# A hybrid attention and FFN block: another step-by-step order of the recurrent chain under the projections, and a rearranged start of the FFN

## The chip, the cores and the metric

The kernel runs on the 8 cores of one Trainium2 chip (two dies of four cores); every core does one sequence of the batch. The metric is device time in microseconds (us) of the slowest core.

Such a program has a slow state in some of its executions, in which the cores of one die, or both, get a lower clock.

## The reference

One layer: a sliding-window attention branch and a gated linear attention branch (GLA) from one input projection, gated and merged, an output projection, and a SwiGLU FFN.

```python
D_MODEL, BATCH, SEQ, FFN_HIDDEN = 2048, 8, 2048, 5632
# 32 query heads of 64, 4 key/value heads, window 128; 4 GLA heads, dk 256, dv 512
u = _rmsnorm(h, norm1_w[l])
proj = u @ w_in[l]
aq, ak, av, gq, gk, gv, g_lr, g_r, gate_a, gate_b = jnp.split(proj, offs, axis=-1)
attn_o = _swa_sink_attention(aq, ak, av, attn_sinks[l])
# S_t = diag(alpha_t) S_{t-1} + k_t^T v_t ; o_t = q_t S_t / sqrt(dk)
gla_o = _gla(gq, gk, gv, log_a)                     # (reshapes left out)
gla_o = _rmsnorm(gla_o, gla_norm_w[l]) * jax.nn.silu(g_r)
h = h + (sigmoid(gate_a) * attn_o + sigmoid(gate_b) * gla_o) @ w_out[l]
v2 = _rmsnorm(h, norm2_w[l])
h = h + (silu(v2 @ w_ffn_gate[l]) * (v2 @ w_ffn_up[l])) @ w_ffn_down[l]
# after the layer: final RMSNorm
```

## The kernel before

Each core handles its sequence in two halves of 1024 tokens (`c` = 0, 1; 8 row tiles of 128 each). In a half, four heads follow one another: 16 attention projections (`a_proj`), then 32 projections for the GLA (`g_proj`), each 16 matmuls of 128x512, some 3.5 us. Under these the kernel lays short dependent chains: the attention chain under `g_proj`, and the GLA chain of a head under the attention projections of the *next* head. Chains and projections are generators; one `next()` emits one step.

The steps of the GLA chain give TensorE 0.23 or 1.30 us of work, but between two of its steps VectorE and ScalarE must do theirs (the row factor, the row `g_gn`), and then TensorE transposes `g_gn`. The weave spreads 19 steps over 16 projections:

```python
def weave(filler, overlay, n_fill, n_over):
    done = 0
    i = 0
    for _ in filler:
        i += 1
        want = min(n_over, (i * n_over) // n_fill)     # 19/16: two steps at i = 6, 11, 16
        while done < want:
            next(overlay, None)
            done += 1

gc = iter(())
for h in range(4):
    weave(a_proj(c, h), gc, 16, 19)
    for _ in gc:
        pass
    if c > 0:
        load(G["g_U"]..., sd[h], "ul", ("sd", h))      # this head's saved state
    ac, gp, gc = a_chain(c, h, range(NT)), g_proj(c, h), g_chain(c, h)
    if h < 3:
        weave(gp, ac, 32, 16)
# head 3: 24 projections with the attention chain (cut), then 8 with the GLA chain
for i in range(8):
    next(gp)
    next(gc)
...
rows_in(range(1, 5))                                   # residual rows of x, 1 MB a tile
dg = d_groups(c)                                       # output projection: one group = 16 matmuls + add
for i in range(11):
    next(gc, None)
    ...
    next(dg)
```

`d_groups` takes its column groups in the order (0, rows 0 to 3), (1, rows 0 to 3), (0, rows 4 to 7), and so on. While it does the last column groups it normalises finished rows (`norm_rows`, VectorE) and transposes them (`norm_turn`: TensorE transposes, ScalarE copies into `v2T`).

The FFN multiplies by Strassen's scheme: seven products `m` per pair of hidden blocks, each twice (`q` = 0, 1) with 8 matmuls; sums of weights (`wsum_part`) and of activations (`xs_add`) are VectorE's. The first pair starts while the last rows are still being normalised:

```python
def snap(bank):
    y = fbuf()                      # the first two of these lie on n2bc, the norm weights
    acopy(y[:], bank[:, :])
    return y

for m in order:                     # first pair: 4, 2, 5, 1, 3, 7, 6
    for q in range(2):
        if m == 4:
            product(A[q], wv[1][:, :, q, 1, :], xs4[:], True)
            m4[q] = snap(A[q])
        elif m == 2:
            product(B[q], wsx[:, 2, :, q, :], v[:, lo, t1], True)
            vtt(m4[q][:], B[q][:, :], m4[q][:], ALU.add)
            out(q, m4[q], 1, t1)    # Silu at q == 0
        elif m == 5:
            product(B[q], wsx[:, 1, :, q, :], v[:, hi, t2], True)
            m5[q] = snap(B[q])
        ...
```

The softmax here doesn't subtract the row's maximum and nothing guards it: scores larger than these inputs give would overflow.

## Time and profile before

| | before |
|---|---|
| median of 4 runs | 3921.66 us |
| fastest of them | 3680.57 us |
| profiled run, slowest core | 3694.52 us (span 3693.0) |
| spans of the 8 cores in it | 3652.6 to 3693.0 us |
| TensorE busy, slowest core | 3591.7 us (97%) |
| half-clock spells between 100 and 3580 us, all 8 cores | 50, costing 15.4 us a core |

The last row is from the clock records of all cores: a spell at half clock costs half its length. The slices round the clock to tenths, so spells of a few microseconds cannot be seen there.

### The profile page before, as it was taken

What the parts mean: (1) busy time and instruction counts of PE and PEld (TensorE: products, weight loads), DVE (VectorE), ACT (ScalarE), POOL (GpSimd) and SP (SyncE); (2) the same over time, 40 slices, a digit from 0 to 9 for tenths busy, and PEclk for the clock granted to TensorE, in tenths of its full rate; (3) what the DMA queues carried; (4) which work ended last, traced back from release to release, by engine and by line L of the source; (5) the groups of instructions that cost most, each with busy time, mean ns of one, the idle gap of its engine ahead of it and who ended that gap; (6) DMA issues with size and microseconds to landing.
All of it is one profiled execution on the core that took longest, in us unless ns stands there. A gap on an engine that the chain in (4) does not pass through costs nothing.

```text
span 3693.0 us, 47906 instructions; the slowest of 8 cores (3652.6 to 3693.0 us)
## 1 busy us (share of the span) xinstructions
PE 3591.7 (97%) x17464; PEld 1630.6 (44%) x17464; DVE 1620.1 (44%) x2589; ACT 1183.5 (32%) x2229; POOL 205.2 (6%) x370
## 2 busy tenths in 40 slices
PE   7999999999999999999999999999999999999997
PEld 5444444444444444444454444444444444444443
DVE  3134443444466513664113343444446674156623
ACT  3153544445333300221113535353533221012212
POOL 1000000000000000000000000000001000000000
PEclk8899999999999999999999999999999999999999
DMA  8344434355666688665954333333456577854464
GB/s 190 50 64 75 68 56 66 51 94 113 160 133 139 108 183 177 138 143 134 218 123 77 61 75 69 69 60 67 92 135 177 120 170 156 200 130 91 89 151 134
DMA packets 110907, 425.35 MB, mean 115 GB/s; under 512 B 13521, under 2 KB 19281, under 8 KB 75089
## 3 DMA queue, kind: packets, MB, share of 16 engines
q0 software_dynamic: 37584, 268.58, 41.3%
q1 hardware_dynamic: 73090, 153.69, 13.0%
q8 instruction: 142, 2.33, 0.3%
q14 instruction: 91, 0.75, 0.1%
HBM read 616.34 MB, written 65.02 MB: 185 GB/s over the span
## 4 chain that ended last, share of the span: by engine, by line
PE 88%; DMA 5%; DVE 3%; ACT 1%; issue 1%; POOL 1%; DVEq 0%; ACTq 0%; POOLq 0%; SPq 0%
PE ps L336 63%; PE ps L877 24%; DMA xnd<-sqh 2%; DMA sq<-xT 1%; PE ps L344 1%; PE ps L632 1%; DMA xr<-x 1%; DMA sq<-x 1%; DVE ws L369 0%; DVE fb L369 0%; DVE mT L380 0%; ACT tt L360 0%; DVE g_gn L380 0%; DVE g_U L380 0%; ACT g_Sb L360 0%
## 5 line engine op out<-in xcount | busy, mean ns | idle before, releaser
L336 PE MATMUL ps<-xnT,wu 128*128 128x512 bf16 (+1 forms) x3264 | 737.9, 384 | 7.9 <-DMA wu<-wmix 4.7
L336 PE MATMUL ps<-wu,xnT 128*128 128x512 bf16 (+1 forms) x3328 | 720.0, 375 | 0.0
L336 PE MATMUL ps<-wu,ff 128*128 128x512 bf16 x2816 | 608.4, 379 | 0.0
L336 PEld LDWEIGHTS ps<-xnT,wu 128*128 128x128 bf16 x3264 | 320.3, 100 | 401.8 <-issue 88.9
L336 PEld LDWEIGHTS ps<-wu,xnT 128*128 128x128 bf16 x3328 | 320.4, 99 | 384.6 <-issue 56.1
L336 PEld LDWEIGHTS ps<-wu,ff 128*128 128x128 bf16 x2816 | 275.4, 98 | 332.4
L877 PE MATMUL ps<-v2T,ws 128*128 128x512 bf16 x1408 | 323.8, 384 | 13.5 <-DVE ws L369 10.4
L877 PE MATMUL ps<-xs,wu 128*128 128x512 bf16 x1408 | 318.2, 379 | 3.2 <-DVE fb L369 2.6
L877 PE MATMUL ps<-v2T,wu 128*128 128x512 bf16 x1408 | 312.5, 379 | 8.1 <-DVE fb L369 5.1
L363 ACT COPY fb<-ps 128x512 f32<-128x512 f32 x264 | 150.5, 582 | 526.6 <-PE ps L877 517.9
L360 ACT ACTIVATE sg<-fb 128x512 bf16<-128x512 f32 x176 | 110.9, 630 | 552.3 <-DVE fb L369 551.0
L369 DVE TENSOR_TENSOR fb<-ps,fb 128x512 f32<-128x512 f32 x264 | 177.9, 688 | 158.9 <-PE ps L877 149.1
L336 PE MATMUL ps<-wu,mT 128*128 128x512 bf16 x1024 | 228.3, 382 | 0.0
L369 DVE TENSOR_TENSOR hy<-ps,hy 128x512 f32<-128x512 f32 x84 | 58.1, 692 | 380.2 <-PE ps L336 380.2
L877 PEld LDWEIGHTS ps<-v2T,ws 128*128 128x128 bf16 x1408 | 138.5, 99 | 183.9 <-issue 22.5
L877 PEld LDWEIGHTS ps<-v2T,wu 128*128 128x128 bf16 x1408 | 137.1, 98 | 176.3 <-issue 12.7
L877 PEld LDWEIGHTS ps<-xs,wu 128*128 128x128 bf16 x1408 | 137.2, 98 | 170.0 <-issue 5.9
L369 DVE TENSOR_TENSOR ws<-wu,wu 128x2048 bf16<-128x2048 bf16 x132 | 160.4, 1218 | 0.1
L877 PE MATMUL ps<-xs,ws 128*128 128x512 bf16 x704 | 159.1, 379 | 0.0
L336 PEld LDWEIGHTS ps<-wu,mT 128*128 128x128 bf16 x1024 | 100.2, 99 | 119.3 <-issue 4.7
L360 ACT ACTIVATE a_t<-a_t 128x512 f32<-128x512 f32 x128 | 80.6, 629 | 202.0 <-DVE a_t L380 195.8
L369 DVE TENSOR_TENSOR ff<-fb,sg 128x512 bf16<-128x512 f32 x176 | 121.8, 692 | 39.1 <-DVE fb L369 22.6
(140 smaller groups left out, 2831.9 us busy)
## 6 DMA issues: line engine op xcount, KB each, us to landing
wu<-wmix POOLq DMA_DIRECT2D x116, 1024.0 KB, 12.6
wu<-wffn POOLq DMA_DIRECT2D x88, 1024.0 KB, 10.8
wu<-wdn POOLq DMA_DIRECT2D x32, 1024.0 KB, 11.8
hy<-h1d SPq DMA_DIRECT2D x84, 256.0 KB, 13.3
h1d<-hy SPq DMA_DIRECT2D x56, 256.0 KB, 9.9
wu<-wdn POOLq DMA_DIRECT2D x16, 768.0 KB, 10.5
xr<-x POOLq DMA_DIRECT2D x8, 1024.0 KB, 29.4
h<-x SPq DMA_DIRECT2D x8, 1024.0 KB, 8.1
```

Of the source, the lines that this page charges most:

```text
L336: r = e.matmul(o_, lhsT=l_, rhs=r_, start=s0, stop=s1)
L344: r = e.transpose(out=o_, in_=i_, identity=identb[:])
L360: S.op("act", lambda e: e.activation(out=o_, in_=i_, func=func, scale=scale, **kw), outs, ins)
L363: S.op("act", lambda e: e.copy(out=o_, in_=i_), [o_], [i_])
L369: S.op("dve", lambda e: e.tensor_tensor(out=o_, in0=a, in1=b, op=op), [o_], [a, b])
L632: r = e.matmul(o_, lhsT=l_, rhs=r_, start=s0, stop=s1)
L877: r = e.matmul(bank[:, :], lhsT=w[:, k, :], rhs=x[:, k, :], start=first and k == 0, stop=k == 7, skip_group_check=True)
```

## The change

It takes no work away and adds next to none. It wants to take away the places where TensorE stands. Its three parts:

1. **Heads.** One chain step per projection, never two. To fit, a chain starts in the last `g_proj` step of its own head and ends in the first three `g_proj` steps of the next.
2. **Hand-off from head 3 to the output projection.** The chain starts one projection earlier; weights are released before the last yield; the output projection does rows 0 to 2 of two column groups first, so late rows of `x` are wanted later.
3. **Start of the FFN.** The first snapshots get buffers of their own; a dummy Silu calls the activation table early; one weight sum goes ahead of the last row norm; one of the last two transposed copies goes to VectorE; the next pair's weight sums move behind the products.

```diff
-            weave(a_proj(c, h), gc, 16, 19)
-            for _ in gc:
-                pass
-            ...
+            for _ in a_proj(c, h):
+                next(gc, None)
             ac = a_chain(c, h, range(NT))
-            ...
+            own = g_chain(c, h)
+            for i, _ in enumerate(g_proj(c, h)):
+                if i < 3:
+                    next(gc, None)
+                if i == 3:
+                    state_in(h)
+                if h < 3:
+                    if i % 2:
+                        next(ac, None)
+                    if i == 31:
+                        next(own)
+                    continue
+                ...                                  # attention chain, loads
+                if i >= 23:
+                    next(own)
+            gc = own
         rows_in(range(1, 5))
         dg = d_groups(c)
-        for i in range(11):
+        for i in range(12):
+            next(dg)
             next(gc, None)
-            if i == 8:
+            if i == 7:
                 rows_in(range(5, 8))
-            next(dg)
+            if i == 10:
+                act(junk[:, 0:1], zcol[:], AF.Silu)
@@ g_proj
+            if i == NT - 1:
+                drop(units)
             yield
-        drop(units)
@@ d_groups
-        for g, ts in ((0, lo), (1, lo), (0, hi), (1, hi), (2, lo), ...
+        for g, ts in ((0, lo[:3]), (1, lo[:3]), (0, lo[3:]), (1, lo[3:]), (0, hi), (1, hi), (2, lo), ...
                     if t == NT - 1:
                         xs_add(c, 1, 4)
+                        wsum_part(c, 0, 5)
                         norm_rows(*rows[0])
@@ norm_turn
-            acopy(v2[c][...], ...)
+            (vcopy if both and q == 0 else acopy)(v2[c][...], ...)
@@ e_half
+    m4s = [place("m4s%d" % i, [128, 512], F32, rM + (28 + 2 * i) * 1024) for i in range(2)]
-                        m4[q] = snap(A[q])
+                        m4[q] = snap(A[q], m4s[q] if j == 0 else None)
                 at = ((7, 0), (7, 1), (6, 0), (6, 1), (6, 1)) if first else ...
+                if first:
+                    at = ((7, 0), "s1", "s5", "s7", "s6")    # all "s" go behind (6, 1)
@@ hooks of the first pair
-                (2, 1): [lambda: norm_turn(c, NT - 1), wp(5), xa(1, 6), wp(1)],
-                (5, 1): [xa(3, 4), xa(3, 6)], (1, 0): [xa(7, 4)], (1, 1): [xa(7, 6), wp(7)],
-                (3, 0): [xa(6, 4)], (3, 1): [xa(6, 6), wp(6)]}):
+                (2, 1): [lambda: norm_turn(c, NT - 1, True), xa(1, 6), wp(1)],
+                (5, 1): [xa(3, 4), xa(3, 6)], (1, 0): [xa(7, 4)], (1, 1): [xa(7, 6), wp(7), wp(6)],
+                (3, 0): [xa(6, 4)], (3, 1): [xa(6, 6)]}):
```

More of the change, by code (lines that the diff above doesn't have):

```diff
@@ L238, in build_nc @@
         ("junk", [128, 512], BF16), ("ss", [128, 32], F32), ("ssx", [128, NT, 4], F32), ("rsx", [128, NT], F32),
-        ("st", [128, 8, 16], F32), ("mhalf", [128, 16], F32), ("rfin", [128, 8, 16], F32),
+        ("st", [128, 8, 16], F32), ("mhalf", [128, 16], F32), ("zcol", [128, 1], F32), ("rfin", [128, 8, 16], F32),
     ]
@@ L247, in build_nc @@
     ss, ssx, rsx, st, mhalf, rfin = (P[n] for n in ("ss", "ssx", "rsx", "st", "mhalf", "rfin"))
+    zcol = P["zcol"]
     n1c = cols_sb[:, 0:16]
@@ L465, in build_nc @@
     vset(declast[:], 0.0)
+    vset(zcol[:], 0.0)
     def first_norm(t):
@@ L747, in g_chain @@
         yield
-    def weave(filler, overlay, n_fill, n_over):
-        done = 0
-        i = 0
-        for _ in filler:
-            i += 1
-            want = min(n_over, (i * n_over) // n_fill)
-            while done < want:
-                next(overlay, None)
-                done += 1
     def norm_stat(t):
@@ L768, in norm_rows, with norm_turn @@
         stt(xn[t % 2][:], h1t[:], r, n2bc[:], ALU.mult, ALU.mult)
-    def norm_turn(c, t):
+    def norm_turn(c, t, both=False):
         for q in (1, 0):
@@ L775, in norm_turn @@
                    for j in range(8)])
-            acopy(v2[c][:, q * 8:(q + 1) * 8, t * 128:(t + 1) * 128], bv.rearrange("p (a b) -> p a b", a=8))
+            (vcopy if both and q == 0 else acopy)(v2[c][:, q * 8:(q + 1) * 8, t * 128:(t + 1) * 128],
+                                                  bv.rearrange("p (a b) -> p a b", a=8))
     def d_groups(c):
@@ L784, in d_groups @@
         rows, turn = [], []
-        for g, ts in ((0, lo), (1, lo), (0, hi), (1, hi), (2, lo), (3, lo), (2, hi), (3, hi)):
+        for g, ts in ((0, lo[:3]), (1, lo[:3]), (0, lo[3:]), (1, lo[3:]), (0, hi), (1, hi), (2, lo), (3, lo), (2, hi),
+                      (3, hi)):
             if g not in held:
@@ L888, in pair, with snap @@
             hc = 2 * (j - j0)
-            def snap(bank):
-                y = fbuf()
+            def snap(bank, y=None):
+                y = y or fbuf()
                 acopy(y[:], bank[:, :])
@@ L951, in e_half @@
                 at = ((7, 0), (7, 1), (6, 0), (6, 1), (6, 1)) if first else ((5, 1), (3, 0), (3, 1), (7, 0), (7, 1))
+                if first:
+                    at = ((7, 0), "s1", "s5", "s7", "s6")
                 for k, fns in nxt(j + 1, at[:4]).items():
+                    k = (6, 1) if isinstance(k, str) else k
                     hk[k] = list(hk.get(k, ())) + fns
-                hk[at[4]] = list(hk.get(at[4], ())) + [lambda j=j: wsum_part(c, j + 1, 6)]
+                k = (6, 1) if first else at[4]
+                hk[k] = list(hk.get(k, ())) + [lambda j=j: wsum_part(c, j + 1, 6)]
             yield from pair(j, (4, 2, 5, 1, 3, 7, 6) if first else (4, 2, 1, 5, 3, 7, 6), hk)
@@ L1156, in rows_in, with state_in @@
                 load(h1[t][:], x[r0:r0 + 128, :], "hx%d" % t)
+        def state_in(h):
+            if c > 0:
+                load(G["g_U"][:, :, :].rearrange("p a b -> p (a b)"), sd[h], "ul", ("sd", h))
         gc = iter(())
         for h in range(4):
-            weave(a_proj(c, h), gc, 16, 19)
-            for _ in gc:
-                pass
-            if c > 0:
-                load(G["g_U"][:, :, :].rearrange("p a b -> p (a b)"), sd[h], "ul", ("sd", h))
-            ac = a_chain(c, h, range(NT))
@@ L1166, in build_nc @@
-            gp = g_proj(c, h)
-            gc = g_chain(c, h)
-            if h < 3:
-                weave(gp, ac, 32, 16)
-        for i in range(24):
-            next(gp)
-            if i % 3 < 2:
-                next(ac)
-            if i == 15:
-                rows_in([0])
-        for _ in ac:
-            pass
-        load(n2bc[:], n2b, "n2")
-        if c + 1 < NCH:
-            acopy(khalo[:], kT[:, :, TT - 128:TT])
-            acopy(vhalo[:], vt[:, NT - 1, :])
-        for i in range(8):
-            next(gp)
-            next(gc)
@@ L1185, in build_nc @@
-        for _ in gp:
-            pass
+            for _ in a_proj(c, h):
+                next(gc, None)
+            ac = a_chain(c, h, range(NT))
+            own = g_chain(c, h)
[10 more added lines that the diff above has]
+                    continue
+                if i < 24 and i % 3 < 2:
+                    next(ac, None)
+                if i == 15:
+                    rows_in([0])
+                if i == 24:
+                    for _ in ac:
+                        pass
+                    load(n2bc[:], n2b, "n2")
+                    if c + 1 < NCH:
+                        acopy(khalo[:], kT[:, :, TT - 128:TT])
+                        acopy(vhalo[:], vt[:, NT - 1, :])
+                if i >= 23:
+                    next(own)
@@ L1204, in build_nc @@
         for _ in e_half(c, 0, {
-                (4, 1): [lambda: norm_turn(c, NT - 2)], (2, 1): [lambda: norm_turn(c, NT - 1), wp(5), xa(1, 6), wp(1)],
-                (5, 1): [xa(3, 4), xa(3, 6)], (1, 0): [xa(7, 4)], (1, 1): [xa(7, 6), wp(7)],
-                (3, 0): [xa(6, 4)], (3, 1): [xa(6, 6), wp(6)]}):
+                (4, 1): [lambda: norm_turn(c, NT - 2)],
+                (2, 1): [lambda: norm_turn(c, NT - 1, True), xa(1, 6), wp(1)],
+                (5, 1): [xa(3, 4), xa(3, 6)], (1, 0): [xa(7, 4)], (1, 1): [xa(7, 6), wp(7), wp(6)],
+                (3, 0): [xa(6, 4)], (3, 1): [xa(6, 6)]}):
             n += 1
```

## The prediction

> **What bounds the kernel now.** I began with the cores, because eight of them can be in different states. All times below are for a fast run, with both dies near full clock: the profiled one took 3694.52 us and the fastest timed one 3680.57. The median of 3921.66 holds slow runs, and I do not predict those.
>
> ```profile
> core 2: 3652.6 us, clock 0.994
> core 4: 3693.0 us, clock 0.985
> ```
>
> Core 4 sets the time. Its stretch from 100 to 150 us ran at a granted clock of 0.81, and core 2's clock record has no such stretch, so most of the 40 us between them is clock that the change does not touch. Next the page: engines and slices.
>
> ```profile
> PE 3591.7 (97%) x17464; PEld 1630.6 (44%) x17464; DVE 1620.1 (44%) x2589; ACT 1183.5 (32%) x2229; POOL 205.2 (6%) x370
> PEclk8899999999999999999999999999999999999999
> ```
>
> TensorE is the bound. The diff adds and removes no matmul; it can win only TensorE's idle time, 3693.0 - 3591.7 = 101 us, and the half-clock spells after it. Some 27 us of that lie before the weights arrive and 20 after the last matmul; about 54 remain. The waits of TensorE say whom it waits for:
>
> ```profile
> PE ps L344 <- DVE g_gn L380: 34.2, 19, 4.3
> PE ps L877 <- DVE fb L369: 10.8, 12, 2.3
> PE ps L877 <- DVE ws L369: 10.4, 2, 5.2
> ```
>
> The first is the linear-attention chain (GLA), the other two the start of the FFN. In the timeline of TensorE, in the GLA chain of head 0 under the projections of head 1:
>
> ```profile
> 302.65 0.28 PE L344 MATMUL ps<-identb,g_ki 128*128 128x128 bf16 x2
> 304.65 0.38 PE L344 MATMUL ps<-identb,g_gn 128*128 128x128 bf16 x4 [1.73 <-DVE g_gn L380]
> ...
> 326.38 0.28 PE L344 MATMUL ps<-identb,g_ki 128*128 128x128 bf16 x2
> 328.75 0.38 PE L344 MATMUL ps<-identb,g_gn 128*128 128x128 bf16 x4 [2.10 <-DVE g_gn L380]
> ...
> 345.39 0.39 PE L344 MATMUL ps<-identb,g_gn 128*128 128x128 bf16 x4
> ```
>
> Here two chain steps stand with no projection between them. The old weave spreads 19 steps over 16 projections, so at the 6th, 11th and 16th it emits two at once. Where there is one projection per step (345.39) there is no wait. The same timeline at the end of head 3, then of all engines at the start of the FFN:
>
> ```profile
> 884.42 0.28 PE L344 MATMUL ps<-identb,g_ki 128*128 128x128 bf16 x2
> 888.99 0.59 PE L344 MATMUL ps<-identb,g_gn 128*128 128x128 bf16 x4 [4.30 <-DVE g_gn L380]
> ...
> 891.51 5.09 PE L336 MATMUL ps<-wu,mT 128*128 128x512 bf16 x16
> ```
>
> ```profile
> 1021.97 1.07 ACT L363 COPY fb<-ps 128x512 f32<-128x512 f32 x2 [4.22 <-DVE xn L380]
> ...
> 1024.88 1.28 ACT L360 ACT_TABLE_LOAD   x1
> ...
> 1026.71 1.91 ACT L363 COPY v2T<-ps 128x1024 bf16<-128x1024 bf16 x2
> ...
> 1027.52 1.22 DVE L369 TENSOR_TENSOR ws<-wu,wu 128x2048 bf16<-128x2048 bf16 x1
> ...
> 1029.00 6.28 PE L877 MATMUL ps<-v2T,ws 128*128 128x512 bf16 x16 [5.19 <-DVE ws L369]
> ```
>
> The reader should see one string of delays: ScalarE's snapshot waits 4.22 us because its buffer lies on the norm weights that VectorE still reads; behind it stand the transposed rows, a table load, Silu, and at last the weight sum that TensorE waits for. And 16 matmuls that take 3.62 elsewhere then take 6.28.
>
> **What the Trainium skill says.** "TensorE: Matmul & The Clock Gate", Part 1: The HAM clock gate: the array falls to half clock after an idle window of about 3.4 us and returns after a busy one. The trace agrees in kind: six half-clock spells of 3.4 or 6.8 us in core 4's clock record, each after such gaps. "ScalarE: Activation LUTs", What ACT_TABLE_LOAD costs: 1283 ns for the load and some 1380 ns of drain. The trace has the 1.28 us, but Silu starts at 1026.18, right behind it; I count no drain. "DMA: Bandwidth & Descriptors", Queues, rings and completion order: a DMA engine takes turns between queues. The trace agrees in direction: the weight load issued at 887.94 beside four 1 MB row loads landed after 16.8 us, the one issued at 852.51 after 11.7.
>
> **The change part by part.**
>
> *Heads 0 to 2.* The chain starts in the last g-projection of its own head, takes one step per projection of the next, and ends in the first steps after. No step is doubled. Each doubled pair costs, from start to start, 304.65 - 302.76 = 1.89 and 328.75 - 326.49 = 2.26 us (two short transposes of 0.055 are taken off); 4.15 a head, six heads in the two halves of the sequence: 24.9. The third doubled step costs about 0.4 in some heads: 1 in all. Two half-clock spells of 3.4 us on core 4 (others have up to four) follow these gaps, and each loses half its length: 3.4. Sum 29.
>
> *Head 3 into the output projection.* One step more now lies before the end of the gate projection, so the 4.30 us wait falls between two projections. What stays is a wait like the 0.57 seen at 879.55, where ScalarE is loaded by the sigmoids. From the end of the last gate matmul (884.30) to the end of the first output group (896.43) took 12.1 us; its work at full clock is 0.23 + 1.30 + 3.45 = 5.0; leaving 0.7 of wait, 6.4 saved, and in both halves 12.8. Against it: the second weight unit of the second column group is wanted sooner. It is issued as that last gate matmul ends, and three output groups and the chain steps between take 0.65 + 1.3 + 3.45 + 0.23 + 3.45 + 1.3 + 3.45 + 0.23 = 14.1 us. Before, such a load took 16.8 us in the first half and 14.5 in the second. I expect a new wait of 3 and 1 us, 4 in all. Net 9.
>
> *Start of the FFN.* Five edits act together: own snapshot buffers (no 4.22 wait), the table load ahead of time by a dummy Silu, one weight sum ahead of the last row norm, one of the two last transposed copies on VectorE (such a copy of 128x1024 took 0.69 in the first norm; ScalarE's take 1.01), and the sums for the next pair moved behind the products. I take the first product's start, 1014.95, as fixed. VectorE: weight sum to 1020.0, last norm to 1022.3 (it began at 1019.53 before, held by its row factor, so the sum costs it 0.5), first add to 1022.9. ScalarE: Silu to 1023.7, the copy that matters to 1024.7. TensorE is free at 1023.4 and starts at 1024.9 where it started at 1029.00. That is 1.4 us idle, short of the idle window, so the half clock should go too. From there VectorE's list (copy 0.6, sums of 1.15 each, adds of 0.61) has the operand of the seventh product at 1039.6 against TensorE's 1038.7: 1 us stays. The second pair's sum needs a weight unit that landed at 1042.94; VectorE would stand on it in the first half, and the second pair starts near 1046.0 instead of 1052.07: 6 saved. In the second half the unit came 3 us earlier relative to the products, and I get 9. Sum 15.
>
> The sum is 29 + 9 + 15 = 53 us: core 4 from 3693.0 to 3640, 1.4%. The earlier release of weights within a head and the later state load are off the path.
>
> **The rivals.** *All gaps go:* the summed start-to-start excess of the gaps above 0.7 us is some 57 us on core 2 after the first 100 us, its half-clock spells cost another 14; all of it would be 71 us and 1.9%. Against it speaks that attention waits of 0.8 (four of them) and the seventh product's wait are untouched. *Waits move to DMA:* the output projection waits 3 us or more for weights in each half, VectorE stands on rows that arrive late (the third row tile landed 13.6 us after the gate matmuls ended, now beside weights from the start), and half-clock spells come back. For it speaks the DMA share of 0.8 around 1000 to 1050 and the 14.1 against 16.8; against it that rows 3 and later are now used later, at about 27 us. That leaves 35 us, 1%. *The clock takes it back:* a denser TensorE may be throttled more, as on core 4 at 0.81; 166 us of it cost about 31 us. That would make the two kernels equal.
>
> **Range and chances.** A fast run before is 3680 to 3695; less 53 that is 3627 to 3642, and I predict 3638. The range 3605 to 3675 holds the DMA rival at its top and a run in which no core is throttled early at its bottom. Over 2% needs 74 us, more than all gaps I can name; only clock luck gives it: 0.10. Within 2%: 0.87. Slower: 0.03.
>
> **What would show it.** In the waits of TensorE the GLA line falls from 34.2 to under 5 us, with no 4.3; the wait for the weight sum falls from 5.2 to under 2 each; the half-clock digits around the FFN's start vanish; the table load stands some 5 us or more before the first Silu; and a wait for a weight DMA of 1 to 3 us appears in the output projection. I am wrong if the GLA waits stay (the distance was not the reason), if the second pair of the FFN starts no sooner than 36 us after the first, or if the weight wait passes 5 us.

## The result, and the profile after

| | before | after |
|---|---|---|
| median, runs | 3680.57 us, 15 runs | 3619.81 us, 10 runs |
| range | 3670.55 to 4304.27 | 3614.63 to 4338.96 |
| profiled run, slowest core's span | 3693.0 us | 3620.5 us |
| half-clock spells, all 8 cores | 50 | 5 |
| their cost a core | 15.4 us | 1.1 us |

The ratio of the fast runs is 0.9855 (95%: 0.9833 to 0.9878), so 1.45% faster: within 2%. A ratio is the mean time of one kernel's fast runs over that of the other's in the same rounds, so it is not quite the ratio of the medians above.

First the cores of the kernel after, then the engine row and the clock slices of its page:

```profile
core 1: 3620.5 us, clock 0.996
core 2: 3605.5 us, clock 0.998
```

```profile
PE 3551.5 (98%) x17464; PEld 1620.6 (45%) x17464; DVE 1618.5 (45%) x2592; ACT 1180.4 (33%) x2229; POOL 204.9 (6%) x370
PEclk9999999999999999999999999999999999999999
```

The matmuls are the same 17464, and yet their busy time is 40 us less than before: matmuls at a lower clock count as longer. The two rows are from different cores (4 before, 1 after), and most of the 40 us is core 4's early 0.81 stretch, which cost it some 31 us and which the change did not remove. The 72.5 us between the two spans is therefore not what the change is worth. Before, cores without that stretch had 3652.6 to 3667; after, all are at 3602 to 3621.

The waits of TensorE after (line waited at, releaser: total us, times, longest):

```profile
PE ps L338 <- DMA wu<-wmix: 8.5, 3, 5.2
PE ps L873 <- DVE fb L371: 6.8, 6, 2.8
PE ps L346 <- DVE g_gn L382: 5.3, 6, 1.2
...
PE ps L873 <- DVE v2T L371: 3.4, 2, 1.7
...
PE ps L873 <- ACT v2T L365: 1.8, 2, 0.9
```

The row of the GLA chain (`g_gn`) fell from 34.2 us to 5.3; the row of the weight sum `ws` (10.4) is gone; in its place stand two waits for ScalarE's copy of `v2T` (1.8 together). The other row for `v2T` (3.4) is the wait of the seventh product, one in each half, which before waited for VectorE too (on `wu`, 3.0 together). And there is a wait for weights from DMA, of which 5.2 is at the start of the program and the rest new.

The timeline of TensorE in a head transition after:

```profile
298.23 0.27 PE L346 MATMUL ps<-identb,g_ki 128*128 128x128 bf16 x2
298.34 3.62 PE L338 MATMUL ps<-xnT,wu 128*128 128x512 bf16 x16
301.80 0.39 PE L346 MATMUL ps<-identb,g_gn 128*128 128x128 bf16 x4
```

The step with `g_ki` and the step with `g_gn` have a whole projection (16 matmuls, 3.62 us) between them, and the second has no wait. In the hand-off to the output projection:

```profile
843.05 1.10 POOL L434 DMA_DIRECT2D wu<-wmix  x2 [0.69 <-PE ps L338]
843.37 0.38 PE L346 MATMUL ps<-identb,g_gn 128*128 128x128 bf16 x4 [0.86 <-DVE g_gn L382]
...
860.35 3.61 PE L338 MATMUL ps<-wu,mT 128*128 128x512 bf16 x16 [2.37 <-DMA wu<-wmix]
```

The wait of 4.30 has become short ones, and the fourth output group waits 2.37 us for weights that were issued at 843.05. At the start of the FFN, with the table load well before it, all engines:

```profile
894.30 1.28 ACT L362 ACT_TABLE_LOAD   x1
...
972.89 0.60 ACT L365 COPY m4s<-ps 128x512 f32<-128x512 f32 x1
...
978.30 0.63 ACT L362 ACTIVATE sg<-m4s 128x512 bf16<-128x512 f32 x1 [1.97 <-DVE m4s L371]
978.84 0.99 ACT L365 COPY v2T<-ps 128x1024 bf16<-128x1024 bf16 x1
...
979.98 3.61 PE L873 MATMUL ps<-v2T,ws 128*128 128x512 bf16 x16 [0.92 <-ACT v2T L365]
...
995.65 3.61 PE L873 MATMUL ps<-v2T,wu 128*128 128x512 bf16 x16 [1.70 <-DVE v2T L371]
```

The snapshot no longer waits, the table load starts 84 us before the Silu that needs it, TensorE waits 0.92 us instead of 5.19, and the 16 matmuls after take 3.61 us instead of 6.28. What remains is 1.70 us at the seventh product. The first 50 us of the FFN, by windows (stretch, length, then busy PE, PEld, DVE, ACT, POOL, each with its count, granted clock, DMA share, GB/s), before and after:

```profile
1005.00:1055.00 50.00, 41.99 (x229) 19.97 (x228) 39.89 (x45) 17.24 (x26) 6.24 (x8) 0.93 0.88 196
```

```profile
960.00:1010.00 50.00, 47.20 (x265) 23.00 (x264) 45.47 (x52) 16.86 (x27) 6.24 (x8) 1.00 0.99 207
```

TensorE did 265 matmuls where it did 229, at a granted clock of 1.00 instead of 0.93. VectorE is now busy 91% of this stretch: a second engine is close to being the bound here.

### The profile page after: what moved, and what is told of

Its sections match the earlier page's. It is cut to its first block, busy times and chain, and to the rows that moved or that the text cites. A ratio compares the mean times of both kernels' runs of the same rounds, so it can differ in the third digit from the quotient of the medians.

```text
span 3620.5 us, 47924 instructions; the slowest of 8 cores (3602.2 to 3620.5 us)
## 1 busy us (share of the span) xinstructions
PE 3551.5 (98%) x17464; PEld 1620.6 (45%) x17464; DVE 1618.5 (45%) x2592; ACT 1180.4 (33%) x2229; POOL 204.9 (6%) x370
## 4 chain that ended last, share of the span: by engine, by line
PE 89%; DMA 6%; DVE 2%; issue 1%; ACT 1%; POOL 0%; DVEq 0%; ACTq 0%; SPq 0%; POOLq 0%
PE ps L338 64%; PE ps L873 23%; DMA xnd<-sqh 2%; DMA wu<-wmix 2%; DMA sq<-x 1%; DMA sq<-xT 1%; PE ps L346 1%; PE ps L636 1%; DVE fb L371 1%; DVE ws L371 0%; ACT junk L362 0%; ACT tt L362 0%; DVE a_P L371 0%; POOL rfin L1044 0%; DVE yp L371 0%
## 5 line engine op out<-in xcount | busy, mean ns | idle before, releaser
L338 PE MATMUL ps<-xnT,wu 128*128 128x512 bf16 (+1 forms) x3264 | 719.2, 376 | 8.3 <-DMA wu<-wmix 5.2
L338 PE MATMUL ps<-wu,xnT 128*128 128x512 bf16 (+1 forms) x3328 | 711.5, 371 | 0.0
L362 ACT ACTIVATE g_Sb<-g_U,dec 128x512 bf16<-128x512 f32 x112 | 77.1, 722 | 190.1 <-DVE g_U L382 178.8
## 6 DMA issues: line engine op xcount, KB each, us to landing
hy<-h1d SPq DMA_DIRECT2D x84, 256.0 KB, 14.1
wu<-wdn POOLq DMA_DIRECT2D x16, 768.0 KB, 10.4
```

Of the source, the lines that this page charges most:

```text
L338: r = e.matmul(o_, lhsT=l_, rhs=r_, start=s0, stop=s1)
L362: S.op("act", lambda e: e.activation(out=o_, in_=i_, func=func, scale=scale, **kw), outs, ins)
```

## The experiments

**Theory (from the prediction).** The saving is the sum of three independent parts: no doubled chain steps (29 us), the hand-off less a new wait for weights (9), the FFN's start (15); the half clock goes where the gaps go. **Rivals:** the distance between chain steps is not the reason for the head waits; the waits move to DMA and eat a good part; the clock takes the gain back through throttling, or, the other way, most of the gain is nothing but clock.

For comparison I use "undisturbed cores": in all timed runs of a kernel, those cores whose mean clock is within 0.005 of the top, and the mean of their spans. For before that is 3663.4 us (58 core-spans) in the rounds of the first four experiments and 3664.1 (64) in those of the last two timed ones. Pair-to-pair intervals (from the start of the FFN's first product to that of the second pair's first) are medians over the cores of one profiled run, first and second half of the sequence. The hand-off is taken from the last gate matmul to the end of the seventh output group; it differs by up to 6 us between the cores of one run, and two cores of each profile lack some matmul records in it, so its medians hold to about one microsecond. Every kernel of this section gave correct results.

**1. The heads alone.** The kernel before with only the new order of heads 0 to 2.

```diff
-            weave(a_proj(c, h), gc, 16, 19)
-            for _ in gc:
-                pass
+            for _ in a_proj(c, h):
+                next(gc, None)
+            # in g_proj of h: i < 3: next(gc, None); i == 3: state_in(h); h < 3 and i == 31: next(own)
```

> The kernel before with only the new schedule of heads 0 to 2 (one chain step per projection, first step in the own head, last two in the next g-projections). Theory (distance between chain steps): the waits of TensorE for g_gn fall from 34.2 us to about 10, the two 4.3 us waits at the end of head 3 stay, no half-clock spell stands between 100 and 800 us or 1950 and 2600 us; 29 us saved, ratio to before 0.992 (0.990 to 0.994). Rival (parts act only together, since a wait removed here is paid at the next stage): ratio 0.996 or above, with longer waits in head 3 or the output projection.

Measured: ratio 0.9896 (0.9851 to 0.9941), a little below the expected 0.990 to 0.994; fast runs of 3639.5 to 3642.7 where before had 3672.2 in these rounds (both without the early throttle), undisturbed cores 31.6 us shorter. The waits of TensorE, slowest core:

```profile
PE ps L344 <- DVE g_gn L380: 10.0, 4, 4.3
```

The 34.2 of the GLA chain falls to 10.0, of which two are the waits of 4.3 at head 3; the FFN's 10.4 for `ws` stays untouched, as it should when only the heads change. No half-clock spell stands between 100 and 800 or 1950 and 2600 us on any core, as expected, and the half-clock cost a core fell from 15.4 to 11.5 us. So 31.6 us against the predicted 29, and most of it is gap, not clock.

**2. The FFN's start alone.** The kernel after with the old heads, hand-off and group order.

```diff
-            for _ in a_proj(c, h):
-                next(gc, None)
+            weave(a_proj(c, h), gc, 16, 19)      # and all of the old main loop and group order
             ...
             if i == 10:
                 act(junk[:, 0:1], zcol[:], AF.Silu)   # kept
```

> The kernel before with only the five edits at the start of the FFN. Theory: the wait of 5.2 us for the weight sum goes to about 1 us, no half clock there, and the second pair starts 29 to 31 us after the first instead of 37; 15 to 17 us saved in both halves, ratio 0.9955 (0.994 to 0.997). Rival (the gain hangs on the earlier end of the linear attention): under 5 us saved, ratio 0.999.

Measured: ratio 0.9948 (0.9899 to 0.9998), undisturbed cores 14.6 us shorter. From the first product to the second pair's first it took 29.25 us in both halves, exactly as in the kernel after, against 37.11 and 37.32 before: 7.9 + 8.1 = 16.0. The GLA waits stayed, so the part does not need the other two:

```profile
PE ps L346 <- DVE g_gn L382: 35.3, 19, 4.3
```

**3. The hand-off alone.** The kernel before with the earlier start of head 3's chain, the early release, the new group order and the loop of 12.

```diff
+            if i >= 23:
+                next(gc)
-        for g, ts in ((0, lo), (1, lo), (0, hi), ...
+        for g, ts in ((0, lo[:3]), (1, lo[:3]), (0, lo[3:]), (1, lo[3:]), (0, hi), ...
-        for i in range(11):
-            next(gc, None)
-            next(dg)
+        for i in range(12):
+            next(dg)
+            next(gc, None)
```

> The kernel before with only the new end of head 3 and the new order of the output projection. Theory: the two waits of 4.3 us go, 6.4 us a half, and waits for a weight DMA of 1 to 3 us come; 8 to 9 us saved in all, ratio 0.9977 (0.996 to 0.999). With the other two parts the sum is 53 us, which is the measured 0.9855. Rival (no new DMA wait by itself; the one after the full change comes of the other parts): 12.8 us, ratio 0.9965, no weight wait in the trace.

Measured: ratio 0.9963 (0.9913 to 1.0013), which by itself does not exclude zero; undisturbed cores 9.6 us shorter; lowest runs 3662.9 against 3672.2, 9.3 shorter. From the last gate matmul to the end of the seventh output group it took 34.4 and 33.1 us where it took 37.05 and 37.36: 6.9 us. The two measures differ by 2.7 us, so the size of this part is known to a few microseconds and no better. Waits of TensorE:

```profile
PE ps L336 <- DMA wu<-wmix: 9.7, 3, 5.5
```

The longest wait for `g_gn` is now 2.1 us, not 4.3, and 9.7 - 5.5 = 4.2 us of waiting for weights is there on the slowest core; the 5.5 is at the start. I had predicted 4 us. The wait comes with the hand-off alone, so it is not the other parts' doing.

By undisturbed cores the three parts make 31.6 + 14.6 + 9.6 = 55.8 us. The whole makes 54.7 (experiment 12). The runs are from two chips, each against the kernel before on the same chip. Within 1 us they add up; none eats another.

**4. The dose.** Only one doubled step per head less: 18 steps over 16 projections, and one step after `g_proj`.

```diff
-            weave(a_proj(c, h), gc, 16, 19)
+            weave(a_proj(c, h), gc, 16, 18)
             ...
                 weave(gp, ac, 32, 16)
+                next(gc)
```

> The kernel before, but the first chain step is given to the own head, so 18 steps stand over 16 projections: two doubled steps a head (8th, 16th) instead of three. Theory (a doubled step costs what one projection less of distance costs): one wait of about 2 us per head instead of two, so g_gn waits of about 22 us instead of 34.2, and 12 to 16 us saved, ratio about 0.996. Rival (starting the chain in the own head is what counts): all of the gain of heads 0 to 2, ratio 0.992, waits of about 10 us.

Measured: the interval of the ratio, 0.9975 (0.9913 to 1.0037), says nothing, since both its fast runs had a throttled pair of cores. Its undisturbed cores are 16.6 us shorter, half of the 31.6 of experiment 1. The waits for `g_gn` went from 34.2 us in 19 to 21.8 in 13. One place in the timeline of TensorE that still waits:

```profile
314.01 0.59 PE L336 MATMUL ps<-g_v,g_kt 128*128 128x512 bf16 x2
314.44 0.28 PE L336 MATMUL ps<-g_qd,g_ki 128*128 128x128 bf16 x2
...
314.66 3.62 PE L336 MATMUL ps<-xnT,wu 128*128 128x512 bf16 x16
320.00 0.38 PE L344 MATMUL ps<-identb,g_gn 128*128 128x128 bf16 x4 [1.72 <-DVE g_gn L380]
```

This sharpens the theory. Here the doubled pair is another one: the step that makes the rows (ending with `g_kt`) is followed at once by the next short step (`g_ki`), then comes a projection, and still TensorE waits 1.72 us at the transposes of `g_gn`. So what counts is not the doubled pair itself but the projections between the step that makes the rows and the one that transposes them: two when the steps are evenly laid, one wherever a pair is doubled between them. The same timeline shows the work in between, one after the other from 313.63: 1.71 and 1.40 us on VectorE, the rest of a 1.38 on ScalarE, 0.58 for the squares, then factor and rows until 319.85. That is 6.2 us, and one projection with the short step covers 4.5.

**5. Fill the FFN's wait with matmuls.** The kernel before with two superfluous products (16 matmuls; the bank is cleared by the real product after) put where TensorE waits 5.19 us.

```diff
                     elif m == 5:
+                        if j == 0 and q == 0:
+                            for _ in range(2):
+                                product(B[q], wsx[:, 2, :, q, :], v[:, lo, t1], True)
                         product(B[q], wsx[:, 1, :, q, :], v[:, hi, t2], True)
```

> The kernel before, with 16 more matmuls (the first weight-sum product once again, into the bank that the waited-for product then overwrites) in the 5.2 us gap at the start of the FFN; the result is unchanged. Theory (the slow matmuls after the gap are the clock gate's answer to an idle TensorE): the wait shrinks to about 1.7 us, the 16 matmuls behind it take 3.6 us instead of 6.3, no half-clock spell stands at the FFN's start, and the second pair starts about 34.5 us after the first instead of 37.1. Rival (they are slow because VectorE or the operands are): they stay at 6.3 us, and the second pair at 37.

Timeline of TensorE:

```profile
1007.20 3.61 PE L877 MATMUL ps<-v2T,ws 128*128 128x512 bf16 x16 [1.74 <-DVE ws L369]
```

The waited-for product starts as late as before (14.05 us after the first), but its 16 matmuls take 3.6 us, not 6.28, and the second pair comes after 34.46 us, not 37.11 (predicted 34.5). No half-clock spell stands there on any core. So 2.65 us of this place's loss was clock alone, and *more* work ended sooner. The rest, 5.2 us a place, was waiting. Both the theory's split between gap and clock and the rival of clock alone are decided: clock is the smaller part.

**6. Without the early table load.** The kernel after less the dummy Silu.

```diff
-            if i == 10:
-                act(junk[:, 0:1], zcol[:], AF.Silu)
```

> The changed kernel without the dummy Silu that loads the table ahead. Theory of the prediction (the load stands in ScalarE's list before the copy that TensorE waits for): the waited-for product starts 11.1 us after the first one instead of 9.8, the second pair at 30.5 instead of 29.3. Rival: ScalarE stood idle 1.97 us before that Silu after the change, so the load of 1.28 us fits in there: no difference, 9.8 and 29.3.

All three executions fell in the slow state (in the profiled one cores 4 to 7 had a mean clock of 0.92); I read core 0, whose die was at full clock, as a profile of the place and not as a time:

```profile
981.30 1.28 ACT L362 ACT_TABLE_LOAD   x1 [1.96 <-DVE m4s L371]
982.59 0.63 ACT L362 ACTIVATE sg<-m4s 128x512 bf16<-128x512 f32 x1
...
984.27 5.30 PE L873 MATMUL ps<-v2T,ws 128*128 128x512 bf16 x16 [2.19 <-ACT v2T L365]
```

The load stood 1.96 us waiting for the same operand as the Silu behind it, and only then took its 1.28. ScalarE's idle time before it therefore hides nothing: all 1.28 lie on the path (the waited-for product starts 11.05 us after the first one, not 9.78). TensorE then waits 2.19 instead of 0.92, and its 16 matmuls take 5.30: here the half clock is back after a wait of 2.2 us. It does not come every time. Six cores in each half ran this stretch without a 13/16 throttle; in seven of these twelve places the half clock follows and the second pair comes after 30.8 to 31.0 us, in five it does not (16 matmuls in 3.61 us, after the same wait) and the second pair comes after 30.35. The medians of the six are 30.6 and 30.9 (predicted 30.5), so the early load is worth 1.3 and 1.6 us: 1.1 for the load itself and some 0.5 where the half clock follows.

**7. Without own snapshot buffers.**

```diff
-                        m4[q] = snap(A[q], m4s[q] if j == 0 else None)
+                        m4[q] = snap(A[q])
```

> The changed kernel with the first two snapshots back in the buffers that lie on the norm weights. Theory (this wait heads the string of delays): ScalarE waits about 4 us before the snapshot for the last row norm, the waited-for product starts about 12 us after the first instead of 9.8, the second pair at 31.5, or 33 if the half clock comes back. Rival (the early weight sum alone cured it): 9.8 and 29.3.

Core 0:

```profile
1005.36 1.07 ACT L365 COPY fb<-ps 128x512 f32<-128x512 f32 x2 [4.69 <-DVE xn L382]
...
1009.83 5.30 PE L873 MATMUL ps<-v2T,ws 128*128 128x512 bf16 x16 [3.12 <-ACT v2T L365]
```

The old wait of the snapshot is back (4.69 us, on VectorE reading the norm weights), TensorE waits 3.12 us, and the half clock is back too, on all cores. The second pair comes after 31.8 and 31.6 us (predicted 31.5 to 33; after 33.0 to 33.1 on the three cores where the half clock lasted 6.8 us and not 3.4): the buffers are worth 2.6 and 2.4 us. Its one fast time, 3649.71 us, holds an early throttle on all eight cores and is not used.

**8. Next pair's sums not deferred.**

```diff
-                    at = ((7, 0), "s1", "s5", "s7", "s6")
+                    at = ((7, 0), (7, 1), (6, 0), (6, 1), (6, 1))
-                k = (6, 1) if first else at[4]
+                k = at[4]
```

> The changed kernel with the next pair's weight sums back between the last products of the first pair. Theory (TensorE's next pair waits until VectorE has drained the bank behind these sums): the waited-for product starts at 9.8 us as after the change, but the second pair at 30.4 instead of 29.3, with a wait of over 1 us in front of it. Rival (VectorE has room): 29.3.

The second pair comes after 30.38 us (predicted 30.4), 1.1 later than in the kernel after, because a drain by VectorE that the products need comes behind the sums (core 0):

```profile
997.99 3.62 PE L873 MATMUL ps<-xs,wu 128*128 128x512 bf16 x16 [1.32 <-DVE m4s L371]
```

Taken away one at a time, buffers, table and deferral make 2.6 + 1.3 + 1.1 = 5.0 of the 7.9 us of the first half. The other two edits, the sum moved ahead of the last norm and the copy on VectorE, were not tried alone, so the remaining 2.9 us are not divided.

**9. Rows of x later.** Is the new wait for weights the fault of the row loads issued with them? Rows 3 and 4 are held back until the first output group has been added.

```diff
-        rows_in(range(1, 5))
+        rows_in(range(1, 3))
         ...
+            if i == 0:
+                rows_in(range(3, 5), h1[0][:, 0:512])    # waits for the first add
```

> The changed kernel, but the loads of row tiles 3 and 4 wait for the first output group's sum, so only row tiles 1 and 2 run beside the weight load that the second column group needs. Theory (that weight load is late because it shares the DMA engines with four row loads): it lands some 13 us after its issue instead of 17, the wait for a weight DMA in the output projection (2.4 us in the slowest core) goes below 0.5, and from the last gate matmuls to the eighth output group it takes about 32.5 us in both halves instead of 35.0 and 33.1. Rival (the load takes that long by itself): no change.

No effect: in core 4 the weights took 844.46 to 861.75, 17.3 us, where they took 17.1 in the kernel after (core 1); row tile 2 landed at 861.58, 0.17 us ahead of the weights. Over all cores the medians are 16.8 us in the first half and 13.2 in the second, against 16.9 and 13.8, and 16.5 and 14.1 in the repeat of the kernel after (experiment 12). The hand-off took 34.6 and 32.5 us against 35.0 and 33.1, and 34.8 and 32.9 in the repeat. So rows 3 and 4, queued behind, did not slow the weights; what the weights share the engines with is rows 1 and 2. Whether holding back row 2 would bring the weights earlier I did not try, and it is open.

**10. Old group order.**

```diff
-        for g, ts in ((0, lo[:3]), (1, lo[:3]), (0, lo[3:]), (1, lo[3:]), (0, hi), ...
+        for g, ts in ((0, lo), (1, lo), (0, hi), ...
```

> The changed kernel with the old order of the output projection (four row tiles of the first column group, then four of the second). Theory (the new order trades a weight wait for a worse one on row tile 3, which lands some 26 us after the gate matmuls): no weight wait, but VectorE stands several us on the row tile and TensorE then 3 us or more for a bank or a chain step; last gate matmuls to eighth output group 36 to 38 us instead of 35.0 and 33.1. Rival (the order doesn't matter, rows come in time): 32.5 us, so the old order would be the better one.

Core 0:

```profile
867.05 0.69 DVE L371 TENSOR_TENSOR h1h<-ps,h1h 128x512 f32<-128x512 f32 x1 [5.68 <-DMA h1h<-x]
...
874.03 0.38 PE L346 MATMUL ps<-identb,g_gn 128*128 128x128 bf16 x4 [2.52 <-DVE g_gn L382]
```

With the old order VectorE stands 5.68 us on row tile 3 of `x`; TensorE then waits 1.12 us for the bank and 2.52 for the chain behind it. The hand-off took 38.6 and 35.8 us (predicted 36 to 38), 3.6 and 2.7 more. No core waits for weights. The new order pays: it gives up a wait for weights of about 2 us to escape a longer wait for rows.

**11 and 12. A further step, and the kernel after again.** After has 1.70 us of wait at the seventh product, for an activation sum on VectorE. Moving that sum one product earlier (on top of the edit of experiment 9) should win it; the kernel after unchanged was timed with it on the same chip.

```diff
-                (3, 0): [xa(6, 4)], (3, 1): [xa(6, 6)]}):
+                (3, 0): [xa(6, 4), xa(6, 6)]}):
```

> The changed kernel with the later row loads and, at the start of the FFN, the last in-place add moved ahead of VectorE's next three operations (the seventh product waited 1.7 us for it). Theory: the second pair starts 27.5 us after the first instead of 29.3, the weight wait is gone; 6 to 7 us less than the changed kernel in the undisturbed cores, ratio to before 0.984 against 0.9855. Rival (both waits come back as others): the same as the changed kernel within 2 us.

> The changed kernel itself once more, on the same chip as the last one, so that the two can be compared: 0.9855 of the kernel before (0.983 to 0.988).

```profile
1000.93 3.61 PE L873 MATMUL ps<-xs,wu 128*128 128x512 bf16 x16 [2.39 <-DVE m4s L371]
```

The 1.70 is gone, and a wait of 2.39 us for the drain of `m4s` stands behind it: the second pair comes after 29.6 and 29.25 us where I had expected 27.5. This prediction failed. It fits a stretch in which VectorE's whole list is near the limit (91% busy in the window above), so that this move only chose where TensorE waits. Undisturbed cores: 3611.1 us for it, 3609.4 for the kernel after, ratios 0.9865 (0.9808 to 0.9923) and 0.983 (0.98 to 0.9859). I have no version that beats the kernel after.

The repeat puts the kernel after at 3664.1 - 3609.4 = 54.7 us below before by undisturbed cores, on another run than the one of the result.

## Why the prediction was right or wrong

The class (within 2%) was right, and the measured median of 3619.81 us lies in the range of 3605 to 3675, 18 us below the predicted 3638. The range is no test of the mechanism: from the true starting point of some 3672 us it holds any saving from nothing to 67 us. The parts are the test.

| step | predicted us | measured us | by |
|---|---|---|---|
| heads 0 to 2 | 29 | 31.6 | undisturbed cores, experiment 1 |
| hand-off, net | 9 | 9.6 (6.9 by its interval) | experiment 3 |
| FFN start, first + second half | 6 + 9 | 7.9 + 8.1 | intervals, experiment 2 |
| sum | 53 | 54.7 | undisturbed cores, kernel after |

- **The saving was right, the starting point was not.** The step that failed is "A fast run before is 3680 to 3695". The typical fast run of before without the early 13/16 stretch takes 3670.6 to 3676 us. I took the profiled run and the fastest of only four timed ones, and the profiled one held 31 us of early throttle, which I had seen and priced but left in the base. 3672 less 54 is 3618, which is what the fast runs of after show.
- **Heads.** Right in mechanism and close in size: experiment 1 isolates it and experiment 4 shows the dose. The words "with no projection between them" named the place, but the distance that counts is between making and transposing the rows (experiment 4). The GLA row fell to 5.3 where "under 5" was to be seen, with nothing above 1.2.
- **Hand-off.** The 0.7 us of remaining wait was mis-sized: 0.86 us stand at that place and another 0.88 one output group on. The wait for weights was predicted as 3 and 1 us; it came as 1.9 to 2.6 in seven cores and none in one, and as 0.9 to 1.9 in four cores and none in the others. The two misses are small.
- **FFN.** The step "the second pair's sum needs a weight unit that landed at 1042.94; VectorE would stand on it" was wrong: that unit is the third pair's, and the second pair's had landed at 1034.21. So the first half saved 7.9 and not 6. The seventh product's wait was predicted as 1 us and is 1.7, so the second half saved 8.1 and not 9. Together they make 1 us.
- **Half clock.** The granted clock of the FFN's start rose from 0.93 to 1.00 as told, and more came with it: the cost a core fell by 14.3 us, about a quarter of the saving. One reading was wrong. The prediction took core 4's six spells to follow idle windows of about 3.4 us, but two of them (at 727 and 2338 us) follow waits of 2.10. Over all cores of the kernel before, each of the 32 waits of TensorE above 4 us is followed by a spell, 18 of the 49 between 2.0 and 2.2 us are, and no shorter one is. That the remaining 0.92 brought none was right, but not for being short of 3.4. Singly, the parts took away 3.9, 2.6 and 2.8, together 9.3; why the whole took more is not settled, and spells differ from run to run.
- **Rivals.** The waits did move to DMA in one place, but for 2.6 us at most, and the saving held. The clock did not take the gain back: all eight cores held a mean of 0.996 to 0.998 over the whole span, at 98% busy TensorE, and slow runs were not more frequent than before (3 of 10 against 6 of 15). "All gaps go" (71 us) failed, since the waits of the attention chain and of the seventh product stayed.

## What to carry to other kernels

Before pricing a change, fix the state of the run that it is priced from: an early throttle of one pair of cores put my base nearly 20 us too high, while the saving itself was off by less than 2. When a short dependent chain is laid under large matmul groups, count at each place, not on average, how many groups stand between the step that makes a result and the step that uses it: 19 steps over 16 groups looks almost even, and its doubled places were more than half of what was won here. Where an engine beside the bound is 90% busy in a stretch, moving one of its items may only move the wait, as in experiment 11; there it is better to take work from it.

## What the Trainium skill lacked or had wrong

- **"TensorE: Matmul & The Clock Gate", Part 1: The HAM clock gate.** The page gives an idle window of about 3.4 us for the fall to half clock and a 13/16 clock to be budgeted once three cores of a die run dense matmuls. Here shorter waits brought spells, but not each time: in the kernel before 18 of 49 waits of 2.0 to 2.2 us did, all 32 above 4 us, and none of the shorter ones; in experiment 6 a wait of 2.2 us (2.7 in one place) brought one (16 matmuls in 5.30 us instead of 3.61) in seven of twelve places. And eight dense cores held a mean clock of 0.996 to 0.998 over 3.6 ms in fast runs; in those, 13/16 came on some cores (in one run on all) for 150 to 210 us near the start, or for 9 to 62 us at the end. Some slow runs are what the page describes: in the one of 4338.96 us the four cores of one die had a mean clock of 0.813 to 0.818, and the other die 0.996 to 0.998.
- **"ScalarE: Activation LUTs", What ACT_TABLE_LOAD costs.** The 1283 ns agree (1.28 us). The further 1380 ns of drain did not show: the Silu starts 1.29 us after the start of the load (experiment 6), and before the change the load starts as the copy ahead of it ends (1024.88). That section doesn't say that the load waits for the operand of the activation behind it: it stood 1.96 us here, so ScalarE's idle time hid nothing of it, and a dummy activation earlier did.
- **"DMA: Bandwidth & Descriptors", Queues, rings and completion order.** What it says of engines taking turns between queues is in agreement, but the section gives no figure for what a neighbouring queue costs. A weight load issued behind two 1 MB row loads took 17.3 us, and with two more rows behind these 17.1, so what was queued behind cost nothing that shows.
